# Linear attention with ReLU features, one core: two octets' stores cut into 112 + 8 + 8 rows, and four more gates ahead of the late stores

## The chip, the cores and the metric

One core of a Trainium2 chip runs the whole problem. Times are device microseconds of that core. The kernel before takes 128.0 us (median of 6 runs, 127.88 to 128.12). "Faster" and "slower" mean by over 2%; smaller differences are judged by the 95% interval of the ratio.

## The reference

```python
batch, heads, seq, dim = 8, 12, 512, 64           # Q, K, V float32
Q_feat, K_feat = np.maximum(0, Q), np.maximum(0, K)
KV = np.einsum('bhkd,bhkv->bhdv', K_feat, V)
K_sum = np.sum(K_feat, axis=2)
numerator = np.einsum('bhqd,bhdv->bhqv', Q_feat, KV)
denominator = np.einsum('bhqd,bhd->bhq', Q_feat, K_sum)
return (numerator / (denominator[:, :, :, None] + 1e-10)).astype(np.float32)
```

37.75 MB are read and 12.58 MB written, with little arithmetic on each byte.

## The kernel before

96 heads are worked on in 12 octets of 8. For each octet the GpSimd queue loads 2 x (k, v) and one q, casting float32 to bfloat16 on the way (the k and v of octet 0 come uncast through the sync and scalar queues); TensorE, ScalarE and VectorE do the rest; the sync queue stores 1 MB of results, 128 rows (partitions) of 8 KB. All loads are issued as early as buffers allow. So that stores don't crowd out loads, each of the first seven stores has a *gate* ahead of it in the sync queue: a tiny copy out of the k tile of five octets later, which can't be issued until that tile has been loaded. What the gate copies is never used.

```python
def load_kv(g):
    k_sb[g] = kin.tile([P, R, D], bf16, name="k_sb")
    nc.gpsimd.dma_start(out=k_sb[g].rearrange("p r d -> p (r d)"), in_=Kr[g])
    ...                                            # v the same, q likewise
scratch = consts.tile([1, D], bf16, name="scratch")
...
def store(o, o_sb):
    if o + DELAY < NO:                             # DELAY = 5, NO = 12: octets 0 to 6
        nc.sync.dma_start(out=scratch, in_=k_sb[2 * (o + DELAY)][0:1, 0, :])
    parts = 2 if o == NO - 1 else 1
    n = RQ // parts
    for j in range(parts):
        rs = slice(n * j, n * (j + 1))
        nc.sync.dma_start(out=Or[o].rearrange("p (r d) -> p r d", d=D)[:, rs], in_=o_sb[:, rs])
```

All gates write the one tile `scratch`, so a gate also waits until the gate before it has landed. Below, gate 7 is the gate ahead of the store of octet 7, which is store 7; the last octet is stored in two halves, 11a and 11b.

## Time and profile before

| | before |
|---|---|
| time, median of 6 | 128.0 us |
| profiled span | 126.2 us |
| last VectorE result | 120.0 us |
| last store's landing, first engine / mean / last engine | 122.76 / 124.05 / 125.28 us |
| transfers on the hardware queues (sync and scalar) | 24 |

Two kinds of records of the trace that the page doesn't print are used throughout. A transfer has sixteen completion times, one for each DMA engine, unnamed; I call the first and last of them the early and the slowest engine. All such times come from one profiled execution of a kernel. And each packet has a start, a duration and a queue.

### The profile page before, as it was taken

How to read it: one execution, taken by the hardware profiler on the slowest of the kernel's cores; microseconds unless marked ns; L12 is line 12 of the kernel's file. 1: busy time of each engine (PE TensorE's matmuls, PEld its weight loads, DVE VectorE, ACT ScalarE, POOL GpSimd, SP SyncE). 2: the span in 40 equal slices, each digit the busy share in tenths (PEclk: the TensorE clock that was granted, in tenths of full speed). 3: DMA queues.
4: the chain of work that ended last, by engine and by line, in shares of the span. 5: the costliest groups of instructions: out<-in, count | busy, mean ns of one | idle time of the engine just before them, and what ended most of it. 6: DMA issues, size and time to landing. Idle time of an engine off the chain costs nothing.

```text
span 126.2 us, 4865 instructions
## 1 busy us (share of the span) xinstructions
PE 77.3 (61%) x2112; PEld 68.3 (54%) x2112; DVE 80.6 (64%) x210; ACT 76.9 (61%) x169; POOL 32.1 (25%) x62
## 2 busy tenths in 40 slices
PE   0032917978397956534997647389964793797200
PEld 0041907967386845434986646178953692696100
DVE  3256785698936959673669787528828628774900
ACT  0165891599198798660799949508917925958000
POOL 6902424325243331241143133033113000000000
PEclk9999999999859999996799999955999679769995
DMA  3999999999999999999999999999999999999992
GB/s 106 374 309 213 214 208 209 217 206 218 205 215 209 208 214 324 257 216 325 256 215 301 280 214 281 301 212 214 347 235 216 316 266 216 352 418 410 416 384 104
DMA packets 10757, 32.81 MB, mean 260 GB/s; under 512 B 1392, under 2 KB 1392, under 8 KB 9328
## 3 DMA queue, kind: packets, MB, share of 16 engines
q0 software_dynamic: 8064, 17.83, 73.9%
q1 hardware_dynamic: 2384, 13.63, 27.1%
q10 hardware_dynamic: 288, 1.05, 2.1%
q8 instruction: 16, 0.26, 0.7%
q14 instruction: 5, 0.04, 0.1%
HBM read 37.75 MB, written 12.58 MB: 399 GB/s over the span
## 4 chain that ended last, share of the span: by engine, by line
DMA 32%; PE 27%; issue 13%; ACT 11%; DVE 10%; ACTq 1%; SPq 0%
DMA v_sb<-in_V_dram 25%; PE ps_out L174 13%; PE ps_kv L139 11%; DMA kv_first<-in_K_dram 7%; ACT kvd L146 5%; ACT qt L159 4%; PE ps_qt L153 3%; DVE o_sb L187 3%; DVE qt L121 3%; ACT vo L134 3%; DVE kf L128 2%; DVE vo L130 1%; DVE rec L186 1%; ACTq L267 0%; DVE kvd L118 0%
## 5 line engine op out<-in xcount | busy, mean ns | idle before, releaser
L139 PE MATMUL ps_kv<-vo,kf 128*128 128x130 bf16 x384 | 32.5, 248 | 21.9 <-ACT vo L134 11.7
L174 PE MATMUL ps_out<-kvd,qt 128*32 128x130 bf16 x1536 | 33.7, 243 | 16.7 <-issue 13.3
L139 PEld LDWEIGHTS <-kf 128*128 128x128 bf16 x384 | 27.8, 112 | 25.3 <-DVE vo L130 16.3
L174 PEld LDWEIGHTS <-qt 128*32 128x32 bf16 x1536 | 27.0, 107 | 21.9 <-issue 15.3
L146 ACT CAST kvd<-ps_kv 64x130 bf16<-64x130 f32 x96 | 25.2, 263 | 16.7 <-PE ps_kv L139 14.8
L134 ACT ACTIVATE vo<-v_sb,mask 128x1024 bf16<-128x1024 bf16 x22 | 26.2, 1190 | 13.9 <-DMA v_sb<-in_V_dram 13.8
L187 DVE TENSOR_TENSOR o_sb<-ps_out,rec 128x768 f32<-128x768 f32 (+1 forms) x36 | 31.3, 868 | 1.4
L159 ACT ACTIVATE qt<-ps_qt 128x512 bf16<-128x512 bf16 x48 | 24.8, 603 | 0.3
L128 DVE TENSOR_SCALAR kf<-k_sb,mask 128x1024 bf16<-128x1024 bf16 x44 | 19.1, 476 | 8.6 <-DMA k_sb<-in_K_dram 8.6
L85 POOL DMA_DIRECT2D k_sb<-in_K_dram x22 | 12.8, 583 | 39.1 <-DMA q_sb<-in_Q_dram 24.1
L184 DVE TENSOR_SCALAR den<-ps_out 128x12 f32<-128x12 f32 (+1 forms) x36 | 5.9, 164 | 17.9 <-PE ps_out L174 17.8
L153 PE MATMUL ps_qt<-ident,q_sb 128*128 128x128 bf16 x192 | 15.7, 245 | 2.4 <-issue 2.4
L87 POOL DMA_DIRECT2D v_sb<-in_V_dram x22 | 12.3, 557 | 17.1 <-DMA k_sb<-in_K_dram 7.3
L153 PEld LDWEIGHTS <-q_sb 128*128 128x128 bf16 x192 | 14.0, 112 | 2.6 <-issue 2.5
L130 DVE TENSOR_SCALAR vo<-v_sb,mask 128x1024 bf16<-128x1024 bf16 x22 | 10.6, 481 | 2.1 <-DMA v_sb<-in_V_dram 2.1
L186 DVE RECIPROCAL rec<-den 128x12 f32<-128x12 f32 (+1 forms) x36 | 7.9, 220 | 1.2
L91 POOL DMA_DIRECT2D q_sb<-in_Q_dram x12 | 6.5, 542 | 7.8 <-DMA v_sb<-in_V_dram 4.1
L128 DVE TENSOR_SCALAR kf<-kv_first,mask 128x1024 bf16<-128x1024 f32 x4 | 2.8, 750 | 4.9 <-DMA kv_first<-in_K_dram 4.9
L134 ACT ACT_TABLE_LOAD x1 | 1.3, 1283 | 5.8 <-DMA kv_first<-in_V_dram 5.8
L121 DVE MEMSET qt<- 128x2048 f32 x2 | 3.5, 1765 | 0.8 <-issue 0.8
L134 ACT ACTIVATE vo<-kv_first,mask 128x1024 bf16<-128x1024 f32 x2 | 2.4, 1180 | 2.6 <-DMA kv_first<-in_V_dram 2.6
L130 DVE TENSOR_SCALAR vo<-kv_first,mask 128x1024 bf16<-128x1024 f32 x2 | 1.5, 747 | 0.0
(12 smaller groups left out, 3.5 us busy)
## 6 DMA issues: line engine op xcount, KB each, us to landing
out_dram<-o_sb SPq DMA_DIRECT2D x11, 1024.0 KB, 9.2
q_sb<-in_Q_dram POOLq DMA_DIRECT2D x12, 512.0 KB, 14.9
k_sb<-in_K_dram POOLq DMA_DIRECT2D x22, 256.0 KB, 13.8
v_sb<-in_V_dram POOLq DMA_DIRECT2D x22, 256.0 KB, 13.2
kv_first<-in_V_dram ACTq DMA_DIRECT2D x2, 512.0 KB, 7.3
kv_first<-in_K_dram SPq DMA_DIRECT2D x2, 512.0 KB, 7.0
out_dram<-o_sb SPq DMA_DIRECT2D x2, 512.0 KB, 5.1
scratch<-k_sb SPq DMA_DIRECT2D x7, 0.1 KB, 5.1
```

The lines of the kernel that those rows point to most:

```text
L85: nc.gpsimd.dma_start(out=k_sb[g].rearrange("p r d -> p (r d)"), in_=Kr[g])
L87: nc.gpsimd.dma_start(out=v_sb[g].rearrange("p r d -> p (r d)"), in_=Vr[g])
L128: nc.vector.tensor_scalar(kf[g][:, :, s, :], k_sb[g], scalar1=0.0, scalar2=mask[:, 0, s:s + 1], op0=Alu.max, op1=Alu.mult)
L130: nc.vector.tensor_scalar(vo[g % NB][:, :, 0, 0:D], v_sb[g], scalar1=mask[:, 1, 0:1], scalar2=None, op0=Alu.mult)
L134: nc.scalar.activation(vo[g % NB][:, :, 1, 0:D], v_sb[g], Act.Copy, scale=mask[:, 1, 1:2])
L139: nc.tensor.matmul(ps_kv[g], kf[g][:, r, :, :].rearrange("p s d -> p (s d)"), vo[g % NB][:, r, :, :], start=(r == 0), stop=(r == R - 1), s ...
L146: nc.scalar.copy(kvd[g % NK][64 * c:64 * c + 64, :, s, c, :], ps_kv[g][64 * s:64 * s + 64])
L153: nc.tensor.transpose(ps_qt[o, i][:, u, :], q_sb[o][:, i * (U // 2) + u, :], ident)
L159: nc.scalar.activation(qtz[o % NZ][:, z, us, :, z, :], pv[:, :, :, z, :], Act.Relu)
L174: nc.tensor.matmul(po[hs, b, c:c + 2 * D1], qtf[o % NZ][:, z, u * P + 32 * w:u * P + 32 * w + 32], kvd[(2 * o + h // 4) % NK][:, h % 4 // ...
L186: nc.vector.reciprocal(rec, den)
L187: nc.vector.tensor_tensor(o_sb[:, 2 * u0:2 * (u0 + nu)].rearrange("p (b r) d -> p b r d", b=2), pv[:, :, :, 0:D], rec.unsqueeze(3).to_broa ...
```

## The change

As I read the edit, the intent is balance: some DMA engines finish later than others, so give eight engines a row more, and eight a row fewer, in each of two octets; and let the last loads go ahead of four late stores.

```diff
+    def cuts(o):
+        rows = slice(0, RQ)
+        if o in (1, 3):
+            return [(slice(0, 112), rows), (slice(112, 120), rows), (slice(120, P), rows)]
+        if o == NO - 1:
+            return [(slice(0, P), slice(0, RQ // 2)), (slice(0, P), slice(RQ // 2, RQ))]
+        return [(slice(0, P), rows)]
     def store(o, o_sb):
-        if o + DELAY < NO:
-            nc.sync.dma_start(out=scratch, in_=k_sb[2 * (o + DELAY)][0:1, 0, :])
-        parts = 2 if o == NO - 1 else 1
-        ...
+        if o < NO - 1:
+            late = o + DELAY - NO
+            x = k_sb[2 * (o + DELAY)] if late < 0 else (k_sb, v_sb)[late % 2][NO * 2 - 2 + late // 2]
+            nc.sync.dma_start(out=scratch, in_=x[0:1, 0, :])
+        Ov = Or[o].rearrange("p (r d) -> p r d", d=D)
+        for ps, rs in cuts(o):
+            nc.sync.dma_start(out=Ov[ps, rs], in_=o_sb[ps, rs])
```

Stores 7 to 10 thus get gates too, on the k and v tiles of the last octet.

More of the change, by code (lines that the diff above doesn't have):

```diff
@@ L190, in norm @@
             rec.unsqueeze(3).to_broadcast([P, 2, nu, D]), op=Alu.mult)
-    def store(o, o_sb):
-        if o + DELAY < NO:
-            nc.sync.dma_start(out=scratch, in_=k_sb[2 * (o + DELAY)][0:1, 0, :])
-        parts = 2 if o == NO - 1 else 1
-        n = RQ // parts
-        for j in range(parts):
-            rs = slice(n * j, n * (j + 1))
-            nc.sync.dma_start(out=Or[o].rearrange("p (r d) -> p r d", d=D)[:, rs], in_=o_sb[:, rs])
+    def cuts(o):
[5 more added lines that the diff above has]
+        return [(slice(0, P), rows)]
+    def store(o, o_sb):
+        if o < NO - 1:
[5 more added lines that the diff above has]
+            nc.sync.dma_start(out=Ov[ps, rs], in_=o_sb[ps, rs])
     zero(0)
```

## The prediction

> **What bounds the kernel now.** I read the page's part 2 first, to see which resource is full, and when.
>
> ```profile
> PE   0032917978397956534997647389964793797200
> DMA  3999999999999999999999999999999999999992
> HBM read 37.75 MB, written 12.58 MB: 399 GB/s over the span
> ```
>
> PE is idle part of the time in nearly every slice; DMA stands at 9 from the second slice to the last but one. 50.33 MB through 16 engines are 3.146 MB each; at 8192 B per 0.307 us (below) that is 118 us of a 126.2 us span. So what counts is how many packets an engine carries, how long an engine stands empty, and when the *last* of the 16 is done.
>
> Then the table of stretches, the end cut fine (columns: stretch, length, busy us and count of PE, PEld, DVE, ACT, POOL, granted clock, DMA share, GB/s).
>
> ```profile
> 46.00:106.00 60.00, 41.48 (x1199) 36.64 (x1186) 39.65 (x98) 39.12 (x88) 13.86 (x25) 0.89 1.08 262
> 106.00:112.00 6.00, 4.47 (x119) 3.95 (x119) 4.98 (x14) 5.64 (x14) 0.00 (x0) 0.76 1.05 339
> 112.00:122.00 10.00, 4.91 (x188) 4.09 (x185) 5.53 (x13) 3.12 (x8) 0.00 (x0) 0.97 1.00 415
> 122.00:126.20 4.20, 0.00 (x0) 0.00 (x0) 0.00 (x0) 0.00 (x0) 0.00 (x0) 0.59 0.39 158
> ```
>
> A share over 1 means that packet records overlap slightly. Up to 112 us loads and stores mix; from 112 to 122 only stores run, gaplessly (1.00); after 122 the share is 0.39 with no computing at all. The end is a ragged tail of stores.
>
> How ragged, the trace's completion records say: a DMA has sixteen, one an engine. The last store's lie (from the span's start) at 122.76, .79, .80, .83, .93, 123.40, .53, .97, 124.56, .92, .95, .97, .99, 125.08, .10 and 125.28 us. Eight engines finish at 123.13 on average, eight at 124.98; the mean of all is 124.05, so perfect balance would be worth 125.28 - 124.05 = 1.23 us. Where the lag comes from is in part 3:
>
> ```profile
> q0 software_dynamic: 8064, 17.83, 73.9%
> q1 hardware_dynamic: 2384, 13.63, 27.1%
> q8 instruction: 16, 0.26, 0.7%
> ```
>
> The 16 instruction packets are 16 KB each, take 0.94 us, and come every 6 us from 25 us on. Loads that land before the first show a spread of 0.6 us over their engines; just after it one engine lies 1.28 us behind the next. By 64 us, after seven fetches, some seven engines are 1 to 1.5 us behind; at the end some eight are about 2 us behind and five not at all. Sixteen fetches on eight engines are two each, 1.9 us: that is the lag.
>
> Last, the stores' issue, from the queue engine's timeline and its waits.
>
> ```profile
> 94.66 0.53 SPq L202 DMA_DIRECT2D out_dram<-o_sb  x1
> 104.08 0.50 SPq L197 DMA_DIRECT2D scratch<-k_sb  x1
> 104.67 15.71 SPq L202 DMA_DIRECT2D out_dram<-o_sb  x7
> SPq L197 <- DMA k_sb<-in_K_dram: 71.9, 7, 41.3
> SPq L197 <- DMA scratch<-k_sb: 22.8, 6, 4.3
> ```
>
> A small read of a loaded tile is the gate ahead of each of the first seven stores. It also waits for the gate before it, as all write one scratch tile. After 104.67 us the last five octets' stores are issued ungated, as fast as VectorE delivers, and the queue never runs dry.
>
> **What the Trainium skill says.** *DMA: Bandwidth & Descriptors*, "Why a DMA increments its semaphore by 16 and not by 1": a transfer from the sync queue uses the largest k up to 16 that divides the slowest dimension, and these are the lowest-numbered k engines. So 128 rows are 8 an engine, 112 are 7 an engine, and 8 rows are one each on engines 0 to 7. The trace shows 1408 packets of 8192 B for eleven 128-row stores, which agrees for 128; 112 and 8 don't occur. Same page, "Queues, rings and completion order": an engine takes turns between queues by packet and takes one queue in order. That agrees: while both queues are full, q1's 322 ns packets against q0's 173 ns ones get 10 to 11 of 16 engines. *SBUF — State Buffer*, "Door 1: The DMA port swizzle": bandwidth depends on how many of 16 ports the partitions reach; rows 112 to 119 lie on two ports, 120 to 127 on two others. No run here shows a transfer on so few. *DMA: Bandwidth & Descriptors*, "Latency and other measured facts" calls engines 7 and 15 usually slower; here some eight lag, so that isn't this case's imbalance.
>
> **The change, part by part.** *Split stores.* Per split octet engines 0 to 7 carry 7 + 1 + 1 = 9 rows and 8 to 15 carry 7, instead of 8 each. In the gapless stretch successive stores complete 2.45 us apart on an engine, 0.307 us a row. Two octets shift 2 x 0.307 = 0.61 us off one half onto the other. The records don't name the engines, so whether 0 to 7 are the half without fetches isn't visible; I take the change's choice as a sign that they are, at about 4 to 1. Then the late half ends at 125.28 - 0.61 = 124.67 and the early half's latest at 123.97 + 0.61 = 124.58: the end moves by 0.6. The early half also gets four more 22 ns completion packets, which cost nothing there. The two additional issues per octet, some 0.5 us each, lie in about 8 us in which the queue engine waits anyway.
>
> *Four more gates.* Each is one 8 B and one 4 B packet an engine, 22 to 28 ns each: 4 x 0.05 = 0.2 us as recorded, 0.1 to 0.15 us after overlap. As waits for loads they are empty: the four loads land at 104.06, 105.29, 106.50 and 107.76 us, about when the gated stores would start anyway. What bites is the chain of gates. Gate n sits in the queue behind store n-1; gate n+1 can go only when gate n has landed on all engines; store n+1 goes after it. From the end of store n-1 on the slowest engine: landing 0.4 (last store) to 0.65 us (a gate: packet ends 108.51, lands 109.15), gate issue to store issue 0.60, store issue to first data about 1.1 us when nothing is queued ahead (the first load: issued 0.74, first packet 1.76, so 1.02). Sum 2.1 to 2.4 us, and store n covers 2.45 us. It just fits: a hole of 0 to 0.3 us at each of stores 8, 9 and 10; I take 0.1 each, 0.3 in all, partly outside the path where the slower half has a backlog, so 0.2. Under load the latency is 3.7 us (gate issued 42.87, first packet 46.64), but there loads are ahead of it.
>
> *Sum:* -0.6 + 0.15 + 0.2 = -0.25 us: 128.03 - 0.25 = 127.8.
>
> Computing isn't near the path: the last VectorE result is there at 120.0 us, the store that takes it starts moving after 123 on the late half.
>
> **Rivals.** *A: the wrong half.* If the fetches sit on engines 0 to 7, the same two rows are added to the late half: +0.6 + 0.15 + 0.2, 129.0 us. For it speaks only that the engines can't be told apart; against it that the change would then have no point.
>
> *B: the gates make holes.* If latency with other engines writing stays near 2 us rather than 1.1, the chain takes 3.1 to 3.4 us against 2.45, three holes of 0.6 to 0.9: +1.8 to +2.7, less 0.45, so 129.4 to 130.3. For it: the only latencies seen under load are 3 us and more. Against: the queue is then drained, like at the start.
>
> *C: few ports.* If four engines share a port for an 8-row store, four rows pass in 1.2 us instead of 0.31 (estimate: 4 x 0.307). Unhidden, the early half gets 4 x 1.2 - 2 x 0.31 = +4.2 us and ends near 127.5 instead of 123.1: about 2.2 us later than now, 130.2. Against: these stores fall among loads, which can take the turns.
>
> *D: nothing.* Lag shifts with the timing of the fetches, the gain is lost in the gates: 128.0.
>
> **Range and chances.** My own account (127.2 to 127.9) has about 50%, D 20%, A 13%, B and C together 17%. The upper tail is longer, since three of the four ways add time and perfect balance can't give more than 1.23 us. So 127.8, range 127.2 to 129.5. Faster by 2% would be under 125.5, twice what perfect balance is worth: 1%. Slower by 2% would be over 130.6, which needs B or C in full or both: 6%.
>
> **What would show it.** Part 6: stores of 896 and 64 KB beside the 1024 KB ones, twice as many 64 KB ones. The packet count rises by 4 x 32 for gates and a few dozen completions; bytes don't change. In the stretch from 122 us the DMA share rises while the stretch gets shorter, and the last store's completions lie within about 1 us rather than 2.5 (my account), or over 3 us apart (A). B shows as a share well under 1.00 between 112 and 122 us, with waits of the queue engine on the scratch DMA up by some 8 to 12 us. C shows as 64 KB stores that take much longer than the 896 KB ones to land, or as 8192 B packets far over 322 ns around the second and fourth store. A span down by over 1.2 us would break the balance argument; one up with a share of 1.00 to the end would break the account of the gates.

## More of the kernel before

The page's part 6 lists the transfers by what they carry (times issued, KB each, us from issue to landing):

```profile
out_dram<-o_sb SPq DMA_DIRECT2D x11, 1024.0 KB, 9.2
...
out_dram<-o_sb SPq DMA_DIRECT2D x2, 512.0 KB, 5.1
scratch<-k_sb SPq DMA_DIRECT2D x7, 0.1 KB, 5.1
```

There are 11 + 2 stores and 7 gates. A gate of 128 bytes takes as long to land as a store of 512 KB: it is in the same queue, behind other packets. The sync queue's own waits in the last 4 us (us in total, times, longest):

```profile
SPq L267 <- DMA out_dram<-o_sb: 4.4, 3, 2.0
```

Three waits for three landings (stores 10, 11a and 11b), and then the program ends, 0.91 us after the last landing.

## The result, and the profile after

The changed kernel takes **130.37 us** (median of 6, 129.8 to 130.48) against 128.0: ratio 1.0176, 95% interval 1.0157 to 1.0196. Ratios are the mean time of one kernel's fast runs over that of the other's from the same rounds, so they are not quite the ratio of the medians. It is 2.4 us slower, inside 2% by a little and outside the predicted range.

The DMA row of the page's part 2 (tenths of the engines' time in 40 slices of 3.2 us), which was all 9 before but for the ends:

```profile
DMA  4999999999999999999999999999999999869595
```

The transfers now (view of the DMA queues):

```profile
out_dram<-o_sb SPq DMA_DIRECT2D x9, 1024.0 KB, 8.6
...
out_dram<-o_sb SPq DMA_DIRECT2D x2, 896.0 KB, 9.4
...
out_dram<-o_sb SPq DMA_DIRECT2D x4, 64.0 KB
scratch<-k_sb SPq DMA_DIRECT2D x9, 0.1 KB, 4.9
scratch<-v_sb SPq DMA_DIRECT2D x2, 0.1 KB, 2.3
```

The stretches at the end (columns as in the prediction; the last two are DMA share and GB/s):

```profile
112.00:122.00 10.00, 4.74 (x190) 3.92 (x187) 6.22 (x16) 3.51 (x10) 0.00 (x0) 0.97 0.73 295
122.00:126.20 4.20, 0.00 (x0) 0.00 (x0) 0.00 (x0) 0.00 (x0) 0.00 (x0) 0.50 0.98 397
126.20:128.70 2.50, 0.00 (x0) 0.00 (x0) 0.00 (x0) 0.00 (x0) 0.00 (x0) 0.50 0.43 172
```

From 112 to 122 us, where the engines moved 415 GB/s without a gap before, 27% of their time is now empty. The sync queue's timeline (start, length, what) shows what they wait for:

```profile
104.67 0.50 SPq L209 DMA_DIRECT2D scratch<-k_sb  x1
105.27 0.88 SPq L212 DMA_DIRECT2D out_dram<-o_sb  x1
109.61 0.50 SPq L209 DMA_DIRECT2D scratch<-k_sb  x1
110.20 0.54 SPq L212 DMA_DIRECT2D out_dram<-o_sb  x1
113.62 0.50 SPq L209 DMA_DIRECT2D scratch<-v_sb  x1
114.22 0.53 SPq L212 DMA_DIRECT2D out_dram<-o_sb  x1
116.13 0.50 SPq L209 DMA_DIRECT2D scratch<-k_sb  x1
116.72 0.54 SPq L212 DMA_DIRECT2D out_dram<-o_sb  x1
120.54 0.50 SPq L209 DMA_DIRECT2D scratch<-v_sb  x1
121.14 1.95 SPq L212 DMA_DIRECT2D out_dram<-o_sb  x3
```

Gate, store, gate, store: each pair comes 2.5 to 4.9 us after the one before it, where a store occupies an engine for 2.45 us. The waits name the cause:

```profile
SPq L209 <- DMA scratch<-k_sb: 31.6, 9, 4.5
...
SPq L209 <- DMA scratch<-v_sb: 1.3, 1, 1.3
```

Together 32.9 us against 22.8: 10.1 us more of gates waiting for gates. No wait on the last v loads appears. The loads weren't helped either: the last q load lands on its slowest engine at 112.42 us, before at 111.87.

The end itself looks wholly different. The last store's completions lie within 0.17 us of each other (127.61 to 127.78), where they were spread over 2.51 us. The engines are level, and late.

### The profile page after: what moved, and what is told of

Its sections match the earlier page's. It is cut to its first block, busy times and chain, and to the rows that moved or that the text cites. A ratio compares the mean times of both kernels' runs of the same rounds, so it can differ in the third digit from the quotient of the medians.

```text
span 128.7 us, 4881 instructions
## 1 busy us (share of the span) xinstructions
PE 74.7 (58%) x2112; PEld 65.7 (51%) x2112; DVE 80.7 (63%) x210; ACT 77.2 (60%) x169; POOL 32.2 (25%) x62
## 4 chain that ended last, share of the span: by engine, by line
DMA 35%; PE 30%; DVE 13%; issue 12%; ACT 3%; ACTq 1%; SPq 0%; DVEq 0%
DMA v_sb<-in_V_dram 28%; PE ps_out L174 14%; PE ps_kv L139 12%; DMA kv_first<-in_K_dram 7%; PE ps_qt L153 4%; DVE o_sb L187 4%; DVE kf L128 3%; DVE qt L121 3%; DVE vo L130 2%; ACT vo L134 1%; DVE rec L186 1%; ACT qt L159 1%; ACT kvd L146 1%; DVE den L184 1%; ACTq L277 0%
## 5 line engine op out<-in xcount | busy, mean ns | idle before, releaser
L139 PE MATMUL ps_kv<-vo,kf 128*128 128x130 bf16 x384 | 31.3, 242 | 22.8 <-ACT vo L134 12.1
L139 PEld LDWEIGHTS <-kf 128*128 128x128 bf16 x384 | 26.4, 108 | 25.9 <-DVE vo L130 16.9
L153 PE MATMUL ps_qt<-ident,q_sb 128*128 128x128 bf16 x192 | 14.2, 232 | 3.0 <-issue 2.7
L153 PEld LDWEIGHTS <-q_sb 128*128 128x128 bf16 x192 | 12.6, 105 | 3.3 <-issue 2.8
```

Source lines behind the costliest of these rows:

```text
L139: nc.tensor.matmul(ps_kv[g], kf[g][:, r, :, :].rearrange("p s d -> p (s d)"), vo[g % NB][:, r, :, :], start=(r == 0), stop=(r == R - 1), s ...
L153: nc.tensor.transpose(ps_qt[o, i][:, u, :], q_sb[o][:, i * (U // 2) + u, :], ident)
```

## The experiments

All kernels gave correct results. "Last" is the last store's last completion in the profiled run; "checks" is explained with one_more, the last experiment but one; "transfers" counts those of the sync and scalar queues.

| kernel | median us | ratio to before, 95% | transfers | last, us | checks |
|---|---|---|---|---|---|
| before | 128.0 | | 24 | 125.28 | 1 |
| changed | 130.37 | 1.0157 to 1.0196 | 32 | 127.78 | 1 |
| gates_only | 130.20 | 1.0152 to 1.0191 | 28 | 127.23 | 5 |
| split_only | 128.46 | 1.0010 to 1.0061 | 28 | 125.52 | 5 |
| own_scratch | 128.01 | 0.9994 to 1.0032 | 32 | 125.28 | 1 |
| own_only | 128.40 | 1.0018 to 1.0043 | 28 | 125.55 | 5 |
| gate_k1 | 128.39 | 1.0014 to 1.0051 | 28 | 125.71 | 5 |
| gates_two | 130.22 | 1.0152 to 1.0192 | 26 | 127.41 | 7 |
| gates_one | 128.86 | 1.0051 to 1.0085 | 25 | 125.38 | 8 |
| gates_10 | 128.34 | 1.0008 to 1.0039 | 25 | 125.19 | 8 |
| split_24 | 128.25 | 1.0002 to 1.0044 | 28 | 125.67 | 5 |
| eight_four | 128.57 | 1.0034 to 1.0061 | 32 | 125.91 | 1 |
| four_one | 127.85 | 0.9979 to 1.0004 | 28 | 124.90 | 5 |
| four_two | 128.22 | 0.9999 to 1.0034 | 32 | 125.52 | 1 |
| null_tile | 127.98 | 0.9981 to 1.0023 | 24 | 125.13 | 1 |
| one_more | 128.43 | 1.0017 to 1.0049 | 25 | 125.20 | 8 |
| four_one_8 | 127.69 | 0.9956 to 0.9986 | 32 | 124.87 | 1 |

### One part alone: gates_only and split_only

```diff
 gates_only: the changed kernel without
-        if o in (1, 3):
-            return [(slice(0, 112), rows), (slice(112, 120), rows), (slice(120, P), rows)]
 split_only: the changed kernel with
-        if o < NO - 1:
+        if o + DELAY < NO:
```

> The kernel before with the four late gates and no split stores. Theory 1 (each gate waits for the gate before it, which lies behind a store, so the queue runs dry): the same holes as in the changed kernel, at stores 8, 9 and 10, DMA share between 112 and 122 us well under 0.9, some 10 us more of waits for the scratch DMA, 130.0 to 131.0 us. Theory 2 (the split stores cost the time, by few ports or by rows on a late engine; gates are nearly free): 128.0 to 128.4 us, share 1.00. Theory 3 (the gates wait for late loads, not for each other) expects 130 us or more here as theory 1 does, but with waits named on the loads.

> The split stores of octets 1 and 3, without the four late gates. Theories 1 and 3: a small gain, 127.3 to 127.9 us, the last store's sixteen completions within less than the 2.5 us of before, no hole in the stores at the end. Theory 2: 129.5 us or more.

gates_only gives 130.20 us: the gates alone make nearly the whole loss. In last landings, the changed kernel's 2.50 us are 1.95 with the gates alone and 0.55 more with the split. split_only gives 128.46, neither the gain expected nor the loss of theory 2. So there are two questions: how the gates cost 2.2 us, and why the split gains nothing.

In gates_only the engines are empty at the same place as in the changed kernel (view of stretches; the second row is a piece out of the first):

```profile
112.00:122.00 10.00, 4.04 (x177) 3.22 (x176) 5.17 (x13) 3.12 (x8) 0.00 (x0) 0.89 0.76 310
120.00:121.50 1.50, 0.00 (x0) 0.00 (x0) 0.00 (x0) 0.00 (x0) 0.00 (x0) 0.50 0.07 27
```

For 1.5 us only one engine in sixteen works.

### Take away the gates' chain: own_scratch, own_only

```diff
+    own = [consts.tile([1, D], bf16, name=f"own{i}") for i in range(4)]
...
-            nc.sync.dma_start(out=scratch, in_=x[0:1, 0, :])
+            nc.sync.dma_start(out=own[late] if late >= 0 else scratch, in_=x[0:1, 0, :])
```

> The changed kernel, but each of the four late gates writes a tile of its own, so that it waits for its load alone and not for the gate before it. Theory 1: the holes go, the time is that of the split stores alone plus at most 0.2 us for the small packets, 127.3 to 128.1 us. Theory 2 and theory 3: no change, 130.2 to 130.5 us.

> The kernel before with the four late gates, each writing a tile of its own, and no split stores: what the gates do without their chain. Theory 1: nothing but their small packets, 128.0 to 128.2 us. If holding stores back for loads is worth something (own_scratch was 0.45 us below split_only), 127.5 to 127.7 us.

own_scratch is the changed kernel with four tiles more, and it takes 128.01 us instead of 130.37. A late gate that waits only for its load costs nothing measurable here (ratio to before 0.9994 to 1.0032), so it was the wait for the gate before it. Its stretch and its waits:

```profile
112.00:122.00 10.00, 4.39 (x180) 3.37 (x177) 5.35 (x13) 3.16 (x9) 0.00 (x0) 0.98 1.00 413
```

```profile
SPq L210 <- DMA scratch<-k_sb: 23.2, 6, 4.9
```

The share is 1.00 again and the waits on the scratch tile are six, as before. Theory 3 falls too: these gates still wait for the late loads. own_only, the same without the split, was expected at 128.0 to 128.2 and measured 128.40. This 0.4 us stayed open until one_more.

### How few gates suffice: gates_two, gates_one, gates_10

```diff
 gates_two: gates 7 and 8            gates_one: gate 7
-        if o < NO - 1:              -        if o < NO - 1:
+        if o + DELAY < NO + 2:      +        if o + DELAY < NO + 1:
 gates_10: gate 10 alone
-        if o < NO - 1:
+        if o + DELAY < NO or o == NO - 2:
```

> gates_only with the late gates of stores 7 and 8 alone. In gates_only the slowest engine's completions of stores 6 to 10 were 2.47, 3.11, 3.76 and 2.52 us apart against 2.45: 0.7 us at store 8, 1.3 us at store 9 (a gate held by an instruction fetch), nothing at 7. So 128.0 + 0.7, 128.4 to 128.9 us, with full DMA share near 120 us. If the loss were one of the first gate: 130 us. If only of the fetch: 128.0 to 128.2.

> The kernel before with one late gate, that of store 7. Theory 5 (what the gates do is to hold the early engines until the slowest has come up; once all are level, every later fetch on any engine is added to the end, about 1.5 us, where before an engine with slack took it): one gate holds store 7 until about 111.1 us, the early engines lose 1 us of their 2.5 and keep the rest, the slowest lose nothing, so 128.0 to 128.4 us and completions of the last store still spread over 1.2 us or more. Rival (the first gate of the chain alone brings the loss): 129.5 us or more.

> The kernel before with one late gate, that of store 10, which waits for the last v load and for gate 6, both landed long before. Theory 5 and theory 1: nothing is held, 128.0 to 128.2 us. Rival (a gate among queued stores costs by its own packets or by its write on all engines): 128.4 us or more, as own_only.

gates_two missed its expectation by far: two gates cost 130.22 us, as much as four. After gate 8 its sync queue holds nothing back (timeline):

```profile
113.37 0.50 SPq L207 DMA_DIRECT2D scratch<-v_sb  x1
113.97 6.98 SPq L210 DMA_DIRECT2D out_dram<-o_sb  x5
```

and where gates_only stood empty, its engines are full:

```profile
120.00:121.50 1.50, 0.00 (x0) 0.00 (x0) 0.35 (x1) 0.00 (x0) 0.00 (x0) 0.50 1.07 431
```

So the same loss comes without the conspicuous hole of gates_only at 120 us, which my expectation had counted. The completions say what does. The slowest engine's completion of each store, and at store 8 the early engine's too (us):

```text
              6       7       8 (early, slowest)    9       10      11a     11b
before      112.79  115.26  114.99  117.70         120.15  122.84  124.06  125.28
gates_one   112.64  115.19  115.85  117.64         120.08  122.94  124.16  125.38
gates_two   113.12  116.11  117.87  118.53         122.53  124.98  126.20  127.41
gates_only  112.80  115.27  117.58  118.38         122.14  124.66  125.97  127.23
changed     113.35  115.86  118.10  118.95         122.70  125.22  126.49  127.78
own_scratch 112.95  115.40  114.62  117.88         120.33  122.80  124.05  125.28
```

At store 8 the engines of before are spread over 2.71 us. With two or more chained gates they are within 0.66 to 0.85 us: a gate must land on all sixteen engines, so store 8 is issued only when the slowest engine is through with the stores before it, and the early ones have stood idle until then. That itself costs the slowest engine 0.5 to 0.7 us up to store 8, counted from its store 6. Then, between stores 8 and 10 one more 16 KB instruction packet arrives (before: at 118.6 us; gates_two: at 120.4), and holds one engine up. In gates_two fifteen engines complete store 9 by 120.96 and one at 122.53, 1.57 us later, and nothing after it makes that good. In before, an engine that completes store 9 at 119.13 seems to be the one that completes store 10 at 122.84, which is 1.26 us more than a store's 2.45; as it had been 1.02 us ahead of the slowest, the end moves by 0.24 only. (The records don't name engines; this pairing is the only one I see that leaves all others at 2.45.)

For gates_two the sum over stores, each against before, is 0.33 (store 6) + 0.53 (store 7, where another fetch of 1.73 us falls) - 0.03 (store 8) + 1.55 (store 9) - 0.24 (store 10) - 0.01 (stores 11a and 11b) = 2.13 us, which is the difference of the last landings.

In gates_only and in the changed kernel the packets show the fetch itself at work. Gate 9's packet starts on fifteen engines by 117.63 us (gates_only) and 118.11 us (changed), but on one only at 118.86 and 119.37 us: there a 16 KB packet ends at 118.87 and 119.38 us. Gate 10 and store 10, which wait for gate 9, are issued after that (gate 10 at 119.97 and 120.54 us), so the other engines stand empty near 120 us.

gates_one holds early engines by 0.9 us and leaves them a lead of 1.79 us at store 8; its last landing is 0.10 us later than before. gates_10, a gate that waits for nothing, lands at 125.19; that its time was over the expected 128.0 to 128.2 us is again a matter of one_more. So the loss isn't in proportion to the gates: it comes when the chain has made the engines level. gates_one's time is 0.8 us over before all the same, and over the expected 128.4. Its profiled run, the fastest of four, took 128.49 us, 0.46 over before, of which 0.10 are the landing and the rest the end of the program (one_more, below); the other three runs took 0.3 to 0.5 us longer than that one, and why stays open.

### A gate on one engine: gate_k1

```diff
+            n = D if late < 0 else 1
-            nc.sync.dma_start(out=scratch, in_=x[0:1, 0, :])
+            nc.sync.dma_start(out=scratch[:, 0:n], in_=x[0:1, 0, 0:n])
```

> The kernel before with the four late gates as in gates_only, chained over the same scratch tile, but each moves one element, so by the rule of the largest k it runs on engine 0 alone, an early engine without fetches. Theory 1 in its sharper form (a gate costs because it must land on all sixteen engines, so the slowest one and an engine that is busy with a fetch hold back the stores of all): the chain stays but follows an engine that is 2.5 us ahead, the empty stretch near 120 us is gone, 128.0 to 128.5 us. Rival (the chain itself, landing plus two issues plus latency, is longer than a store's 2.45 us on any engine): still 129.3 us or more.

128.39 us, with the chain as long as in gates_only (four late gates on one tile). The chain follows one engine, which is early; the gates land at 110.96, 114.06, 116.53 and 119.04 us. At store 8 the engines keep a spread of 1.50 us and the last landing is at 125.71 (in the slowest of its four runs, 128.64 us). The stretch that was empty in gates_only is full:

```profile
120.00:121.50 1.50, 0.00 (x0) 0.00 (x0) 0.00 (x0) 0.00 (x0) 0.00 (x0) 0.73 0.99 412
```

The rival, that landing plus two issues plus latency is too long on any engine, falls: with an idle engine a gate's first packet moves 1.16 us after its issue in gates_only and 1.27 us here, and the last three gates land 2.5 us after one another, the pace of the stores.

### Which engines are late: who

Octet 10's store is cut so that its small pieces name engines:

```diff
+        if o == NO - 2:
+            Ov = Or[o].rearrange("p (r d) -> p r d", d=D)
+            nc.sync.dma_start(out=Ov[:, 1:RQ], in_=o_sb[:, 1:RQ])
+            for a, b in ((0, 112), (112, 120), (120, 124), (124, 126), (126, 127), (127, 128)):
+                nc.sync.dma_start(out=Ov[a:b, 0:1], in_=o_sb[a:b, 0:1])
+            return
```

> The kernel before, with the store of octet 10 in pieces: 128 rows without their first 256 B, then the first 256 B of rows in pieces of 112, 8, 4, 2, 1 and 1 rows, which by the rule of the largest k go to engines 0 to 15, 0 to 7, 0 to 3, 0 to 1, and 0. Each piece's completions tell where these engines stand in their queue. If the lower half are the early engines, the 8-row piece lands on all its engines by about 121.5 us while the full store spreads over 120 to 122.5; if the lower half are the late ones, between 121.7 and 122.5; if fetches are mixed over both halves, some of each. Time about 128.0 to 129, of no interest.

The completions (us):

```text
128 rows, all engines   119.89 119.93 119.97 120.06 120.30 120.85 120.86 121.50
                        121.97 122.34 122.38 122.40 122.42 122.50 122.64 122.82
8 rows, engines 0 to 7  120.25 120.34 120.41 121.21 121.21 121.89 122.37 122.92
4 rows, engines 0 to 3  120.42 120.58 121.39 121.40
2 rows, engines 0, 1    120.60 121.57
1 row, engine 0         120.78
```

An engine that two lists share stands in the second about 0.17 us later than in the first (0.36 us from the 128 rows to the 8); so the lists can be matched. An 8-row store has eight completions, plus one at once (in the changed kernel 0.44 to 0.50 us after its issue; left out of the lists) that fills up the semaphore. That agrees with the Trainium skill, *DMA: Bandwidth & Descriptors*, "Why a DMA increments its semaphore by 16 and not by 1": the k engines used count themselves and the sequencer writes the remaining 16 - k immediately. Engine 0 is early and engine 1 some 0.95 us behind; of 2 and 3 one is early and one 0.95 behind; of 4 to 7 one is early and three are 1.6, 2.1 and 2.7 us behind. Of the seven latest (122.34 us and more) six are in the upper half. So **neither half is the early one**, and the engine that ends last may be in the half that the change gives more rows to.

### The split, in other doses: split_24, eight_four, four_one, four_two

```diff
 split_24:   if o in (2, 4):          eight_four: if o in (1, 2, 3, 4):
 four_one:   if o == 1:               four_two:   if o in (1, 3):
 four_one and four_two cut at
+    return [(slice(a, e), rows) for a, e in ((0, 112), (112, 116), (116, 120), (120, 124), (124, P))]
 all four without late gates
```

> split_only with octets 2 and 4 in place of 1 and 3: does the small loss of the split repeat? Theory 4 (a late engine of the lower eight carries two rows more): 128.3 to 128.6 us, with one or two completions of the last store well behind the rest. If the loss was scatter between builds: 127.6 to 128.1.

> No late gates; octets 1 to 4 stored as 112 + 8 + 8 rows, twice the dose of the split. Theory 4: the latest of engines 4 to 7 carries four rows more, 1.23 us, and ends last: 128.8 to 129.3 us, with a few engines far behind the rest. If instead the lower half were early and two octets merely overshot by chance, four octets would push eight engines together to the end. If the loss of split_only was noise: 127.5 to 128.2.

> No late gates; octet 1 alone stored as 112 rows and four times 4 rows, so engines 0 to 3 carry 11 rows and all others 7. The pieces of octet 10 showed engines 0 to 3 at 0, 0, 0.95 and 0.95 us of lag and the latest engines at 2.55 (in 4 to 7) and 2.8 (in 8 to 15). Theory 4 (the lower eight hold late engines too, and rows given to those end last): 0 to 3 end 0.92 later, at most 1.9, all others 0.31 earlier, so 0.2 to 0.35 us faster than before, 127.6 to 127.8. Rival (a store in pieces costs by itself, whichever engines get the rows): 128.2 us or more.

> As four_one, for octets 1 and 3. Theory 4: the two engines of 0 to 3 that lagged 0.95 us end at 0.95 + 1.84 = 2.8, all others 0.61 earlier than before, so the end is again what it was before or 0.1 to 0.2 later: 128.0 to 128.2 us, with the last completions of engines 0 to 3. Rival (pieces cost by themselves): 128.5 us or more.

Two split octets move the last landing by +0.24 us (split_only) and +0.39 (split_24), four by +0.63: the wrong way and growing with the dose, though less than 0.307 a row. In all three, two engines end 0.4 us or more behind all others. Of the expected times, eight_four's (128.57 us) was missed from below, split_24's (128.25) and four_one's (127.85) by 0.05 us.

Two cautions. A last landing is that of one execution: the four builds that don't differ near the end or have one idle gate more (before, null_tile, one_more, gates_10) land between 125.13 and 125.28 us, own_only, whose gates hold nothing back, at 125.55, and split_24's profile is of its slowest run (128.60 us; the other three took 128.20 to 128.28). And own_scratch, which has the split of octets 1 and 3 too, also shows two engines 0.4 us behind all others, but lands at 125.28 as before does. Less 0.06 us for each further check (one_more, below), the medians put the loss by two split octets at 0.0 to 0.3 us (split_24, own_scratch, split_only) and by four at 0.57. What is shown is that the split gains nothing and that four octets lose; the loss by two isn't clear of the scatter. Late computing is not the cause: store 11b is issued at 121.07 us in split_only and 121.97 in eight_four (120.05 before), but on the slowest engine it still completes 1.24 and 1.25 us after 11a, the pace of half a store, so that engine didn't wait for it.

Rows moved to engines 0 to 3 alone go as theory 4 says: one octet brings the last landing to 124.90, 0.38 earlier (expected 0.31), two octets overshoot to 125.52. four_one, with five pieces in place of one store, is no slower than before, so pieces cost nothing measurable by themselves. Rival C of the prediction gets no support either: in the changed kernel the second 8-row store of an octet completes 0.5 to 0.7 us after the first (both lists in order of time), about what a row takes beside loads (0.307 us at 65% of the engine is 0.47), where four rows through one port would be 1.2; and between 58 and 66 us and between 78 and 86 us, where these stores fall, no packet of 8192 B takes over 322 ns, the sign against C that the prediction named.

### The scatter between builds: null_tile, one_more

```diff
 null_tile: before, with four tiles that nothing uses
 one_more: before, with one more tiny transfer at the first gate
+            for y in own if o == 0 else []:
+                nc.sync.dma_start(out=y, in_=k_sb[2 * (o + DELAY)][0:1, 0, :])
```

> The kernel before with four more small tiles that nothing uses, so other addresses and nothing else: the scatter between builds. own_only, which was to cost nothing, measured 0.4 us. If addresses make such differences: anything from 127.7 to 128.5 us; if not, 128.0 within 0.1, and own_only's 0.4 us belong to its gates.

> The kernel before with one more tiny transfer at 43 us, far from the end. In the traces so far the end of the program checks eight semaphores of the hardware queues in a fixed order, 0.06 us each, and the transfers take these eight in turn. With a multiple of eight transfers the last store has the last of them and one check follows its landing; gates_10, with 25, had eight checks after it, and its span ended 1.3 us after the last landing against 0.9. If that is what own_only's and gates_10's 0.3 to 0.4 us are: 128.4 us, with the last landing where it was, at 125.2 to 125.3 us. If not (late gates cost by themselves): 128.0 us.

These other addresses make no difference (127.98 us). A single transfer at 43 us of a span of 126 us makes 0.43 us at the end (128.43), with the last landing where it was. The sync queue's waits in the last microseconds of one_more, to compare with the three of before:

```profile
SPq L270 <- DMA out_dram<-o_sb: 5.1, 1, 5.1
```

The program's end looks at eight semaphores, one after another, in a fixed order. Before, the last store has the eighth: seven checks lie behind earlier landings, and one, 0.06 us, follows the last. With 25 transfers it has the first, so the queue waits once, 5.1 us, and then makes seven more checks of 0.06 us: 0.42 us. The span ends 1.34 us after the last landing here, and in gates_one, and within 0.02 of it in gates_10; with 24 or 32 transfers it is 0.90 to 0.91 in every kernel above. That is own_only's open 0.4 us in the main: four more checks are 0.24 us, and its last landing is 0.27 later.

### A version that beats both: four_one_8

```diff
 four_one, with four tiny transfers at the first gate: 32 in all
+            for y in own if o == 0 else []:
+                nc.sync.dma_start(out=y, in_=x[0:1, 0, :])
```

> four_one, made 32 transfers in place of 28 by four tiny ones at 43 us, so that the last store has the last semaphore again. four_one's last landing was 0.38 us before that of before, while its time was 0.15 us less. With the four checks of 0.06 us gone: 127.5 to 127.7 us, faster than both kernels. If the gain of four_one was scatter: 127.85 to 128.1.

127.69 us against 127.96 of before in the same rounds, 95% interval 0.9956 to 0.9986, and 2.7 us less than the changed kernel. 0.4 us of the 1.23 us of imbalance is gone.

## Why the prediction was wrong

**The bound** was right. DMA is the limit to the end, and the imbalance of 1.23 us capped what the change could gain; four_one_8, with a third of it, is the best that was found.

**"I take the change's choice as a sign that they are"**, that engines 0 to 7 are the half without fetches, was the first step to fail. It took the place of a measurement. The term -0.6 measured +0.24 (split_only) and +0.39 (split_24) in last landings and 0.00 in own_scratch: a gain in none. who shows three of the lower eight among the late ones.

**The chain of gates** was the second step to fail, and the larger one. It was described rightly and mis-sized: the term of 0.2 us measured 1.95 (the last landing of gates_only against that of before). Its parts held: 0.60 us between a gate's issue and the store's, 1.16 us to the first packet where 1.1 was said. What failed is the step from holes to time. I counted a hole of 0 to 0.3 us at each of three stores, on a chain that just fits. But a gate lands when the last of sixteen engines has come to it, so the chain made the early engines wait for the slowest and removed the lead that lets an engine take a fetch for nothing. That cost 0.5 to 0.7 us by store 8, and one later fetch then counted almost in full, 1.3 to 1.6 us. Two gates do that as well as four. That fetches cause the lag was in the prediction; that they go on during the gated stretch was not.

**Rival B** named the right symptom (129.4 to 130.3 us for a measured 130.37; scratch waits up by 10.1 us where 8 to 12 were said; a share of 0.73 where "well under 1.00" was said) for a wrong reason: latency was not near 2 us. It and C together had 17%, and the range ended at 129.5, below most of what B allowed. Rival A is partly true: a late engine gets the rows, but not all eight are late. Rival C is not seen. Two of the rivals' sums are slightly off, without consequence: B's chain, with 2 in place of 1.1 us, comes to 3.0 to 3.3 us, and C's early half to 127.3.

**"An end within about 1 us"** was given as the sign of my own account. The changed kernel shows 0.17 us, because the engines had been made to wait for each other. An even finish doesn't show that balance has been gained; the DMA share before it must be read with it.

**The gates' own packets**, 0.1 to 0.15 us, can't be told from scatter: four unchained gates land at +0.27 us (own_only) and, with the split, at 0.00 (own_scratch), a single one at -0.09 (gates_10). The number of transfers modulo eight wasn't in the prediction; the changed kernel, with 32, doesn't suffer from it.

What is only argued: that a 16 KB packet is what holds the one engine in gates_two, where no gate follows that would show it. In gates_only and the changed kernel the packets show it for gate 9; no run took the fetches away. Open too are the 0.3 to 0.5 us of three of gates_one's runs.

## What to carry to other kernels

A transfer that others wait for is as late as the slowest of the engines it runs on, so a tiny gate on all sixteen, chained over one shared tile, makes every engine wait for the worst; give each gate a tile of its own (130.20 us chained, 128.40 us with own tiles). Engines that are ahead are not waste where irregular work still comes: look for who takes that work before levelling them, and find out which engine is late by small transfers that land on known ones. When builds that ought to be equal differ by tenths of a microsecond, compare the last landing as well as the time, since the end of the program can add to it.

## What the Trainium skill lacked or had wrong

- *Runtime: NRT & Kernel Launch*, "Instruction fetch mechanics", says that instructions come in 16 KiB blocks over a DMA queue and that fetching is mostly hidden. The 16 packets of 16 KB are there, about 0.94 us each; for the engine that issues the instructions they may be hidden, but they run on the same 16 DMA engines, and in this DMA-bound kernel one put a DMA engine 1.26 to 1.57 us behind. The page doesn't give this cost to other transfers, nor on which engines the fetches fall.
- *DMA: Bandwidth & Descriptors*, "Latency and other measured facts", has engines 7 and 15 as the usually slower ones. Here eight of sixteen are 1.8 us or more behind in the last store of the kernel before, and three of the late ones are among 0 to 7 (who).
- *SBUF — State Buffer*, "Door 1: The DMA port swizzle": 8 rows that lie on two ports showed no slowdown beside loads; a second 8-row store completed 0.5 to 0.7 us after the first, and no 8192 B packet there took over 322 ns.
- No page has these checks at a program's end: eight semaphore checks of 0.06 us in a fixed order, so that one more transfer, at 43 us, cost 0.43 us at the end (the whole: 128.43 against 127.96 us).
